# Weights in eight SP chunks cast by VectorE, add loads moved to stage 2, smaller pools: a matmul with scale and add

## The chip, the cores and the metric

The kernel runs on one core of a Trainium2 chip. Its time is device microseconds of one execution; the figures given are medians of several runs, and the profile is of one of them.

## The reference

```python
batch, m, k, n = 16, 512, 1024, 768
def reference(x, weight, scale, add_value):
    return (scale * np.matmul(x, weight) + add_value).astype(np.float32)
```

All arrays are float32, and scale is 0.1. Seen as matrices, x has 8192 rows of 1024, weight is 1024 x 768, and add_value and the output have 8192 rows of 768. So x is 33.6 MB, add_value and the output 25.2 MB each, and the weights 3.1 MB.

## The kernel before

The 8192 rows are 64 blocks of 128, handled in 32 pairs (`B = 2`). Row block b of pair i takes every 64th row, so that each of the 128 partitions reads one run of 8 KB of x for a pair, and one of 6 KB of add_value.

For each pair there are two stages. `stage1` (L102) issues the load of x on SP (L109) and that of add_value on ScalarE's queue (L111). For each of the two blocks VectorE casts x to bf16 (L119), PE transposes it in eight tiles of 128 x 128 into PSUM (L126), and ScalarE moves them to `xt`, four at a time, multiplying by scale (L132). `stage2` (L135) multiplies: for each block PE runs 8 slices of K times two parts of N (512 and 256 columns) into `mm_psum` (L143), VectorE adds `add_t` (L151), and POOL's queue stores the pair (L156).

The loop (L158) calls stage 1 of pair i and then stage 2 of pair i-2 (`DELAY`). The weights come by one transfer on POOL's queue which also casts to bf16, ahead of everything (L70); all product matmuls read this one tile.

How far one engine can run ahead of another is set by the pools: five buffers of a pair each for x, add_value and the output (`XF`, `ADD`, `OUT`), five of a block each for the bf16 x and for `xt` (`XC`, `XT`), two PSUM tiles for transposes and three for products. The order on each engine is worked out by a scheduler from the program and the pools. It puts casts and transposes ahead of the matmuls of an earlier pair, as far as buffers let it. Each engine then works strictly in that order.

Of the kernel before, what the change touches and what calls it, by code (L numbers as in the profile page):

```python
# [2 lines left out]

# [5 lines left out]


@with_exitstack
def kernel(
    ctx: ExitStack,
    tc: tile.TileContext,
    x: bass.AP,
    weight: bass.AP,
    scale: float,
    add_value: bass.AP,
    out: bass.AP,
):  # L20
# [15 lines left out]
    mm_dtype = mybir.dt.bfloat16  # L36

    B = int(os.environ.get("MB", 2))
    XF_BUFS = int(os.environ.get("XF", 5))
    XC_BUFS = int(os.environ.get("XC", 5))  # L40
    XT_BUFS = int(os.environ.get("XT", 5))
    ADD_BUFS = int(os.environ.get("ADD", 5))
    OUT_BUFS = int(os.environ.get("OUT", 5))
    TG = int(os.environ.get("TG", 4))
    SPLIT = int(os.environ.get("SPLIT", 512))
    MM_BUFS = int(os.environ.get("MMB", 3))
    DELAY = int(os.environ.get("DELAY", 2))
    XENG = os.environ.get("XENG", "sync")
    ADDENG = os.environ.get("ADDENG", "scalar")
    OUTENG = os.environ.get("OUTENG", "gpsimd")  # L50
    XCAST = int(os.environ.get("XCAST", 0))
# [10 lines left out]
    identity = const_pool.tile([P, P], mm_dtype)  # L62
    make_identity(nc, identity)

    def eng(name):
        return getattr(nc, name)

    w_view = weight.rearrange("(ko p) n -> p ko n", p=P)
    w_bf16 = const_pool.tile([P, K_SUB, N], mm_dtype)
    nc.gpsimd.dma_start(w_bf16, w_view)  # L70

    xf_pool = ctx.enter_context(tc.tile_pool(name="xf_pool", bufs=XF_BUFS))
    xc_pool = ctx.enter_context(tc.tile_pool(name="xc_pool", bufs=XC_BUFS))
    xt_pool = ctx.enter_context(tc.tile_pool(name="xt_pool", bufs=XT_BUFS))
    add_pool = ctx.enter_context(tc.tile_pool(name="add_pool", bufs=ADD_BUFS))
    out_pool = ctx.enter_context(tc.tile_pool(name="out_pool", bufs=OUT_BUFS))
    psum_t = ctx.enter_context(tc.tile_pool(name="psum_t", bufs=2, space=bass.MemoryType.PSUM))
# [18 lines left out]
    assert o <= PSUM_N  # L96

    xt_tiles = {}
    add_tiles = {}
    fscale = float(scale)  # L100

    def stage1(bi):  # L102
        b0 = bi * B
        if XCAST:
            x_all_bf16 = xf_pool.tile([P, B, K], mm_dtype, tag="x_fp32")
            nc.gpsimd.dma_start(x_all_bf16, x_v[:, b0:b0 + B, :])
        else:
            x_fp32 = xf_pool.tile([P, B, K], mybir.dt.float32, tag="x_fp32")
            eng(XENG).dma_start(x_fp32, x_v[:, b0:b0 + B, :])  # L109
        add_t = add_pool.tile([P, B, N], mybir.dt.float32, tag="add_t")  # L110
        eng(ADDENG).dma_start(add_t, add_v[:, b0:b0 + B, :])  # L111
        add_tiles[bi] = add_t

        for b in range(B):
            if XCAST:
                x_bf16 = x_all_bf16[:, b, :]
            else:
                x_bf16 = xc_pool.tile([P, K], mm_dtype, tag="x_bf16")
                nc.vector.tensor_copy(x_bf16, x_fp32[:, b, :])  # L119

            xt = xt_pool.tile([P, K_SUB, P], mm_dtype, tag="xt")
            for tg in range(T_TILES):
                tpsum = psum_t.tile([P, TG, P], mm_dtype, tag="tpsum")
                for j in range(TG):
                    kt = tg * TG + j
                    nc.tensor.transpose(  # L126
                        tpsum[:, j, :],
                        x_bf16[:, kt * P:(kt + 1) * P],
                        identity,
                    )  # L130
                dst = xt[:, tg * TG:(tg + 1) * TG, :]
                nc.scalar.mul(dst, tpsum, fscale)  # L132
            xt_tiles[(bi, b)] = xt
# [64 lines left out]
```

## Time and profile before

| | us |
|---|---|
| median of 6 runs (254.44 to 255.05) | 254.66 |
| the profiled execution | 255.05 |
| its span, first to last instruction | 253.1 |
| PE busy | 205.8 |
| VectorE busy | 106.9 |
| ScalarE busy | 71.1 |
| weights: transfer under way | 1.31 to 40.1 |

The execution's time is 1.95 us above its span. In the profile's names, PE is the matmul engine, PEld its weight loads, DVE is VectorE, ACT ScalarE, POOL GpSimd, and SP the engine that issues the loads of x; an engine's name with q is its queue. L143 is line 143 of the kernel as printed above. DMA share is the mean busy share of 16 DMA engines; it can go over 1, as packets overlap.

### The profile page before, as it was taken

The numbers are of one execution on the slowest core, as the hardware profiler recorded it, in microseconds if no ns is written. First come the engines' busy times: TensorE is split into PE (matmuls) and PEld (weight loads), VectorE is DVE, ScalarE is ACT, GpSimd is POOL, SyncE is SP. The second block draws the span as 40 slices with busy tenths as digits, with TensorE's granted clock in tenths as the row PEclk, the third lists the DMA queues.
The fourth block names the chain that finished last, engine by engine and source line by source line (L and its number), as shares of the span: only waits on it lengthen the run. The fifth ranks groups of instructions, "written<-read, shape, count | busy, mean of one in ns | idle before, by whom it ended". The sixth has DMA issues, their size and how long they took to land.

```text
span 253.1 us, 3745 instructions
## 1 busy us (share of the span) xinstructions
PE 205.8 (81%) x1506; PEld 130.7 (52%) x1536; DVE 106.9 (42%) x192; ACT 71.1 (28%) x129; POOL 18.9 (7%) x39
## 2 busy tenths in 40 slices
PE   0200006999999999999999999999999999999980
PEld 0200004666666666666666666666666666666640
DVE  0221002555555555555555555555555555433340
ACT  0400003433333333333333333333333333333000
POOL 2000000000000000000000000000000000000000
PEclk9999999999999999999999999999999999999997
DMA  7999992979999999999999999999999878863333
GB/s 258 377 378 377 370 354 82 315 238 417 372 388 420 415 417 415 416 413 419 396 403 424 413 398 414 413 388 414 418 418 412 286 246 247 246 268 124 122 130 124
DMA packets 14881, 85.70 MB, mean 339 GB/s; under 512 B 1552, under 2 KB 2576, under 8 KB 10768
## 3 DMA queue, kind: packets, MB, share of 16 engines
q1 hardware_dynamic: 4608, 33.56, 32.6%
q10 hardware_dynamic: 4608, 25.17, 27.9%
q0 software_dynamic: 5648, 26.74, 27.4%
q8 instruction: 12, 0.20, 0.3%
q14 instruction: 5, 0.04, 0.0%
HBM read 61.87 MB, written 25.17 MB: 344 GB/s over the span
## 4 chain that ended last, share of the span: by engine, by line
issue 60%; PE 17%; DMA 15%; POOL 6%; POOLq 0%; DVE 0%; DVEq 0%
DMA w_bf<-in_weight_dram 15%; PE mm_psum L143 13%; POOL out_dram L156 5%; PE tpsum L126 4%; POOLq L193 0%; DVE out_t L151 0%; POOLq L156 0%; POOL identity masks.py:197 0%; DVEq L119 0%; POOLq masks.py:199 0%; POOLq L179 0%
## 5 line engine op out<-in xcount | busy, mean ns | idle before, releaser
L143 PE MATMUL mm_psum<-w_bf,xt 128*128 128x256 bf16 (+1 forms) x994 | 181.7, 326 | 30.7 <-DMA w_bf<-in_weight_dram 29.2
L143 PEld LDWEIGHTS <-xt 128*128 128x128 bf16 x1024 | 98.0, 98 | 57.3
L132 ACT ACTIVATE xt<-tpsum 128x512 bf16<-128x512 bf16 x128 | 69.8, 594 | 154.7 <-PE tpsum L126 81.8
L151 DVE TENSOR_TENSOR out_t<-mm_psum,add_t 128x512 f32<-128x512 f32 (+1 forms) x128 | 65.4, 553 | 94.4 <-PE mm_psum L143 94.4
L126 PEld LDWEIGHTS <-x_bf 128*128 128x128 bf16 x512 | 38.1, 100 | 57.6 <-issue 44.5
L119 DVE CAST x_bf<-x_fp 128x1024 bf16<-128x1024 f32 x64 | 43.8, 689 | 45.8 <-PE tpsum L126 29.7
L126 PE MATMUL tpsum<-identity,x_bf 128*128 128x128 bf16 x512 | 46.3, 224 | 9.6 <-DVE x_bf L119 8.6
L156 POOL DMA_DIRECT2D out_dram<-out_t x32 | 17.1, 535 | 228.1 <-DVE out_t L151 228.1
L132 ACT ACT_TABLE_LOAD x1 | 1.3, 1283 | 8.4 <-DMA add_t<-in_add_value_dram 8.4
L70 POOL DMA_DIRECT2D w_bf<-in_weight_dram x1 | 1.0, 1033 | 0.4 <-issue 0.4
masks.py:199 POOL TENSOR_SCALAR_AFFINE_SELECT identity<-identity 128x128 bf16<-128x128 bf16 x1 | 0.3, 306 | 0.1
masks.py:197 POOL MEMSET identity<- 128x128 bf16 x1 | 0.2, 206 | 0.3 <-POOLq L179 0.3
L179 POOL MEMSET const-float32-0.0<- 128x1 f32 x1 | 0.1, 100 | 0.2 <-issue 0.2
L179 POOL MEMSET const-uint8-127<- 128x1 uint8 x1 | 0.1, 103 | 0.0
L179 POOL MEMSET const-bfloat16-1.0<- 128x1 bf16 x1 | 0.1, 102 | 0.0
L179 POOL MEMSET const-float32-1.0<- 128x1 f32 x1 | 0.1, 100 | 0.0
## 6 DMA issues: line engine op xcount, KB each, us to landing
x_fp<-in_x_dram SPq DMA_DIRECT2D x32, 1024.0 KB, 10.7
add_t<-in_add_value_dram ACTq DMA_DIRECT2D x32, 768.0 KB, 10.1
out_dram<-out_t POOLq DMA_DIRECT2D x32, 768.0 KB, 10.2
w_bf<-in_weight_dram POOLq DMA_DIRECT2D x1, 1536.0 KB, 38.8
```

The source lines that it names most:

```text
L70: nc.gpsimd.dma_start(w_bf16, w_view)
L119: nc.vector.tensor_copy(x_bf16, x_fp32[:, b, :])
L126: nc.tensor.transpose(tpsum[:, j, :], x_bf16[:, kt * P:(kt + 1) * P], identity,)
L132: nc.scalar.mul(dst, tpsum, fscale)
L143: nc.tensor.matmul(mm_psum[:, poffs[si]:poffs[si] + nlen], xt[:, kt, :], w_bf16[:, kt, n0:n0 + nlen], start=(kt == 0), stop=(kt == K_SUB - 1),
L151: nc.vector.tensor_add(out_t[:, b, n0:n0 + nlen], mm_psum[:, poffs[si]:poffs[si] + nlen], add_t[:, b, n0:n0 + nlen],)
L156: eng(OUTENG).dma_start(out_v[:, bi * B:(bi + 1) * B, :], out_t)
L179: nc = _bacc.Bacc("TRN2", target_bir_lowering=False, num_devices=1)
```

## The change

- Weights: the one casting transfer on POOL's queue is gone. There are eight chunks of 128 x 768 in float32, each with tiles of its own (`wf`, `wb`), loaded on SP (L89) and cast to bf16 by VectorE (L111). Chunk 0 is issued behind x of pair 0, chunks 1 to 7 behind x of pair 1.
- add_value: its load is no longer part of stage 1. `load_add` comes ahead of stage 2 of the same pair; the first three go on SP, the others on ScalarE's queue (L148).
- Pools: x from 5 to 3 buffers, bf16 x from 5 to 3, `xt` from 5 to 4, add_value from 5 to 3, output from 5 to 4.
- `DELAY` is 1 where it was 2.
- Stores of the last six pairs go on SP where the others go on POOL's queue (L211).
- Switches that are read from the environment are added; with their defaults they change nothing else.

```diff
-    XF_BUFS = int(os.environ.get("XF", 5))
-    XC_BUFS = int(os.environ.get("XC", 5))
-    XT_BUFS = int(os.environ.get("XT", 5))
-    ADD_BUFS = int(os.environ.get("ADD", 5))
-    OUT_BUFS = int(os.environ.get("OUT", 5))
...
-    DELAY = int(os.environ.get("DELAY", 2))
...
+    XF_BUFS = _env("XF", 3)
+    XT_BUFS = _env("XT", 4)
+    ADD_BUFS = _env("ADD", 3)
+    OUT_BUFS = _env("OUT", 4)
...
+    DELAY = _env("DELAY", 1)
...
-    w_bf16 = const_pool.tile([P, K_SUB, N], mm_dtype)
-    nc.gpsimd.dma_start(w_bf16, w_view)
...
+        for kt in range(K_SUB):
+            wf = const_pool.tile([P, N], fp32, tag=f"wf{kt}")
+            wb = const_pool.tile([P, N], mm_dtype, tag=f"wb{kt}")
...
+        def load_weight_chunk(kt):
+            nc.sync.dma_start(w_fp32[kt], w_view[:, kt, :])
...
+                nc.vector.tensor_copy(w_bf16[kt], w_fp32[kt])
...
-    xc_pool = ctx.enter_context(tc.tile_pool(name="xc_pool", bufs=XC_BUFS))
+    xc_pool = ctx.enter_context(tc.tile_pool(name="xc_pool", bufs=_env("XC", 3)))
...
+    def load_add(bi):
+        add_t = add_pool.tile([P, B, N], fp32, tag="add_t")
+        e = nc.sync if bi < ADD_BUFS else eng(ADDENG)
+        e.dma_start(add_t, add_v[:, bi * B:(bi + 1) * B, :])
+        add_tiles[bi] = add_t
...
-        add_t = add_pool.tile([P, B, N], mybir.dt.float32, tag="add_t")
-        eng(ADDENG).dma_start(add_t, add_v[:, b0:b0 + B, :])
-        add_tiles[bi] = add_t
...
-                        w_bf16[:, kt, n0:n0 + nlen],
+                        w_bf16[kt][:, n0:n0 + nlen],
...
+        if bi >= N_BATCH - _env("OLAST", 6):
+            oe = os.environ.get("OLASTENG", "sync")
+        eng(oe).dma_start(out_v[:, bi * B:(bi + 1) * B, :], out_t)
...
     for bi in range(N_BATCH + DELAY):
         if bi < N_BATCH:
             stage1(bi)
+            if WINTER and wk < K_SUB:
+                load_weight_chunk(wk)
+                cast_weight_chunk(wk)
+                wk += 1
         if bi >= DELAY:
-            stage2(bi - DELAY)
+            if WINTER and bi == DELAY:
+                while wk < K_SUB:
+                    load_weight_chunk(wk)
+                    cast_weight_chunk(wk)
+                    wk += 1
+            load_add(bi - DELAY)
```

On SP at the start of the program, five loads of x stood one after the other before, as many as there are buffers (`x_fp_86` is pair 0, `x_fp_120` pair 1, and so on):

```order
L109 DMA x_fp_86<-in_x_dram 128x2048
L109 DMA x_fp_120<-in_x_dram 128x2048
L109 DMA x_fp_154<-in_x_dram 128x2048
L109 DMA x_fp_228<-in_x_dram 128x2048
L109 DMA x_fp_302<-in_x_dram 128x2048
```

Now the weight chunks and three loads of add_value stand among them (`x_fp_100` is pair 0, `x_fp_134` pair 1, `x_fp_222` pair 2):

```order
L154 DMA x_fp_100<-in_x_dram 128x2048
L89 DMA wf<-in_weight_dram 128x768
L154 DMA x_fp_134<-in_x_dram 128x2048
L89 DMA wf<-in_weight_dram 128x768 x7
L148 DMA add_t<-in_add_value_dram 128x1536
L154 DMA x_fp_222<-in_x_dram 128x2048
L148 DMA add_t<-in_add_value_dram 128x1536
L154 DMA x_fp_296<-in_x_dram 128x2048
```

What moved: the third load of x stands behind all the weights and the first load of add_value, which were on other queues.

On PE at the second slice of K of the very first block, the matmul before read the one weight tile (`w_bf16_63`), as did the one ahead of it:

```order
L126 MATMUL tpsum_114<-identity_58,x_bf16_105 128x128
L143 LDWEIGHTS xt_92
L143 MATMUL mm_psum_189<-w_bf16_63,xt_92 128x256
L143 LDWEIGHTS xt_92
L143 MATMUL mm_psum_189<-w_bf16_63,xt_92 128x512
```

Now it reads a chunk of its own (`wb_64` is chunk 0, `wb_66` chunk 1):

```order
L170 MATMUL tpsum_126<-identity_58,x_bf16_117 128x128
L194 LDWEIGHTS xt_104
L194 MATMUL mm_psum_183<-wb_64,xt_104 128x256
L194 LDWEIGHTS xt_104
L194 MATMUL mm_psum_183<-wb_66,xt_104 128x512
```

The place in the row is the same; what the matmul needs is now one cast of VectorE, where it was the whole transfer.

On VectorE in the long stage, the cast of the first block of pair 14 (`x_fp32_1042`) stood ahead of the adds of pair 9 (`out_t_854`):

```order
L119 CAST x_bf16_987<-x_fp32_968 128x1024
L119 CAST x_bf16_1046<-x_fp32_1042 128x1024
L151 TENSOR_TENSOR out_t_854<-mm_psum_855,add_t_674 128x512
L151 TENSOR_TENSOR out_t_854<-mm_psum_855,add_t_674 128x256
L151 TENSOR_TENSOR out_t_854<-mm_psum_874,add_t_674 128x512
```

Now it is the cast of the first block of pair 8 (`x_fp32_666`) that stands ahead of the adds of pair 5 (`out_t_552`):

```order
L159 CAST x_bf16_609<-x_fp32_592 128x1024
L159 CAST x_bf16_668<-x_fp32_666 128x1024
L202 TENSOR_TENSOR out_t_552<-mm_psum_553,add_t_550 128x512
L202 TENSOR_TENSOR out_t_552<-mm_psum_553,add_t_550 128x256
L202 TENSOR_TENSOR out_t_552<-mm_psum_572,add_t_550 128x512
```

The row is of the same kind; the casts now lead the adds by three pairs where they led by five.

## Rows read from the trace of the kernel before

**Rows 1.** The page: its span, PE's busy time, and PE in 40 slices
```profile
span 253.1 us, 3745 instructions
...
PE 205.8 (81%) x1506; PEld 130.7 (52%) x1536; DVE 106.9 (42%) x192; ACT 71.1 (28%) x129; POOL 18.9 (7%) x39
...
PE   0200006999999999999999999999999999999980
```

**Rows 2.** The chain of waits: start us, us, what
```profile
1.31 38.80 DMA w_bf<-in_weight_dram
40.14 0.59 PE mm_psum L143
40.73 0.43 PE tpsum L126 x4
...
50.36 0.45 PE tpsum L126 x8
...
141.17 0.53 POOL out_dram L156
...
147.56 0.53 POOL out_dram L156
...
237.02 0.53 POOL out_dram L156
...
242.23 0.53 POOL out_dram L156
```

**Rows 3.** Waits: who for whom, us in total, times, longest
```profile
PE mm_psum L143 <- DMA w_bf<-in_weight_dram: 29.2, 1, 29.2
```

**Rows 4.** Windows: stretch, its us, busy by engine, clock, DMA share, GB/s
```profile
0.00:4.00 4.00, 0.00 (x0) 0.00 (x0) 0.00 (x0) 0.00 (x0) 1.75 (x7) 1.00 0.55 164
4.00:6.00 2.00, 0.00 (x0) 0.00 (x0) 0.00 (x0) 0.00 (x0) 0.00 (x0) 1.00 1.02 424
10.00:40.00 30.00, 0.58 (x4) 0.42 (x4) 2.59 (x4) 1.40 (x3) 0.00 (x0) 1.00 1.03 363
32.00:36.00 4.00, 0.00 (x0) 0.00 (x0) 0.00 (x0) 0.00 (x0) 0.00 (x0) 1.00 1.04 342
56.00:66.00 10.00, 9.90 (x78) 6.31 (x79) 5.66 (x10) 3.26 (x6) 1.07 (x2) 1.00 1.02 421
80.00:200.00 120.00, 118.96 (x889) 75.54 (x904) 63.14 (x114) 41.06 (x76) 10.15 (x19) 1.00 1.01 408
```

**Rows 5.** Waits of SP's queue: us in total, times, longest
```profile
SPq L109 <- DVE x_bf L119: 154.3, 26, 19.2
```

**Rows 6.** Timeline of the start: start us, us, engine, line, operation, idle before
```profile
7.88 1.29 DVE L119 CAST x_bf<-x_fp 128x1024 bf16<-128x1024 f32 x2 [7.88 <-DMA x_fp<-in_x_dram]
```

**Rows 7.** The page: DMA queues q1 (x), q10 (add_value), and the casts of x
```profile
q1 hardware_dynamic: 4608, 33.56, 32.6%
q10 hardware_dynamic: 4608, 25.17, 27.9%
...
L119 DVE CAST x_bf<-x_fp 128x1024 bf16<-128x1024 f32 x64 | 43.8, 689 | 45.8 <-PE tpsum L126 29.7
```

**Rows 8.** Timeline of the last 8 us
```profile
246.10 1.02 DVE L151 TENSOR_TENSOR out_t<-mm_psum,add_t 128x512 f32<-128x512 f32 x2 [1.58 <-PE mm_psum L143]
247.42 0.53 POOL L156 DMA_DIRECT2D out_dram<-out_t  x1 [4.67 <-DVE out_t L151]
```

**Rows 9.** DMA queues in 248 to 252 us: packets, MB, share
```profile
q0 software_dynamic: 144, 0.79, 48.2%
```

**Rows 10.** DMA issues in 80 to 120 us: KB each, median us to landing
```profile
x_fp<-in_x_dram SPq DMA_DIRECT2D x6, 1024.0 KB, 10.1
add_t<-in_add_value_dram ACTq DMA_DIRECT2D x6, 768.0 KB, 9.6
```

**Rows 11.** DMA issues in 0 to 10 us
```profile
x_fp<-in_x_dram SPq DMA_DIRECT2D x5, 1024.0 KB, 17.1
```

**Rows 12.** DMA packets in 10 to 40 us
```profile
DMA packets 2374, 10.88 MB, mean 363 GB/s; under 512 B 192, under 2 KB 1106, under 8 KB 1553
```

More of the change, by code (lines that the diff above doesn't have):

```diff
@@ L50 @@
     OUTENG = os.environ.get("OUTENG", "gpsimd")
-    XCAST = int(os.environ.get("XCAST", 0))
+    TCEV = os.environ.get("TCEV", "scalar")
+    WCAST = os.environ.get("WCAST", "vector")
+    WSCALE = _env("WSCALE", 0)
+    WCHUNK = _env("WCHUNK", 1)
     assert M_TILES % B == 0
@@ L60 @@
     const_pool = ctx.enter_context(tc.tile_pool(name="const", bufs=1))
-    identity = const_pool.tile([P, P], mm_dtype)
+    XBF = _env("XBF", 1)
+    identity = const_pool.tile([P, P], mm_dtype if XBF else fp32)
     make_identity(nc, identity)
@@ L66, in eng, with load_weight_chunk, cast_weight_chunk @@
         return getattr(nc, name)
+    fscale = float(scale)
     w_view = weight.rearrange("(ko p) n -> p ko n", p=P)
-    w_bf16 = const_pool.tile([P, K_SUB, N], mm_dtype)
-    nc.gpsimd.dma_start(w_bf16, w_view)
+    w_bf16 = []
+    w_fp32 = []
+    if WCHUNK:
+        for kt in range(K_SUB):
+            wf = const_pool.tile([P, N], fp32, tag=f"wf{kt}")
+            wb = const_pool.tile([P, N], mm_dtype, tag=f"wb{kt}")
+            w_fp32.append(wf)
+            w_bf16.append(wb)
+        def load_weight_chunk(kt):
+            nc.sync.dma_start(w_fp32[kt], w_view[:, kt, :])
+    else:
+        wf = const_pool.tile([P, K_SUB, N], fp32, tag="wf")
+        wb = const_pool.tile([P, K_SUB, N], mm_dtype, tag="wb")
+        for kt in range(K_SUB):
+            w_fp32.append(wf[:, kt, :])
+            w_bf16.append(wb[:, kt, :])
+        nc.sync.dma_start(wf, w_view)
+        def load_weight_chunk(kt):
+            pass
+    def cast_weight_chunk(kt):
+        if WCAST == "scalar":
+            nc.scalar.mul(w_bf16[kt], w_fp32[kt], fscale if WSCALE else 1.0)
+        elif WCAST == "gpsimd":
+            nc.gpsimd.tensor_copy(w_bf16[kt], w_fp32[kt])
+        else:
+            if WSCALE:
+                nc.vector.tensor_single_scalar(
+                    w_bf16[kt], w_fp32[kt], fscale, op=mybir.AluOpType.mult)
+            else:
+                nc.vector.tensor_copy(w_bf16[kt], w_fp32[kt])
     xf_pool = ctx.enter_context(tc.tile_pool(name="xf_pool", bufs=XF_BUFS))
-    xc_pool = ctx.enter_context(tc.tile_pool(name="xc_pool", bufs=XC_BUFS))
+    xc_pool = ctx.enter_context(tc.tile_pool(name="xc_pool", bufs=_env("XC", 3)))
     xt_pool = ctx.enter_context(tc.tile_pool(name="xt_pool", bufs=XT_BUFS))
@@ L76 @@
     out_pool = ctx.enter_context(tc.tile_pool(name="out_pool", bufs=OUT_BUFS))
-    psum_t = ctx.enter_context(tc.tile_pool(name="psum_t", bufs=2, space=bass.MemoryType.PSUM))
+    psum_t = ctx.enter_context(tc.tile_pool(name="psum_t", bufs=T_BUFS, space=bass.MemoryType.PSUM))
     psum_mm = ctx.enter_context(tc.tile_pool(name="psum_mm", bufs=MM_BUFS, space=bass.MemoryType.PSUM))
@@ L81 @@
     T_TILES = K_SUB // TG
+    SPLIT = 512
     splits = []
@@ L99 @@
     add_tiles = {}
-    fscale = float(scale)
+    evict_mul = 1.0 if WSCALE else fscale
+    def load_add(bi):
[3 more added lines that the diff above has]
+        add_tiles[bi] = add_t
     def stage1(bi):
         b0 = bi * B
[L104 to L109, printed above, removed]
-        add_t = add_pool.tile([P, B, N], mybir.dt.float32, tag="add_t")
-        eng(ADDENG).dma_start(add_t, add_v[:, b0:b0 + B, :])
-        add_tiles[bi] = add_t
+        x_fp32 = xf_pool.tile([P, B, K], fp32, tag="x_fp32")
+        eng(XENG).dma_start(x_fp32, x_v[:, b0:b0 + B, :])
         for b in range(B):
-            if XCAST:
-                x_bf16 = x_all_bf16[:, b, :]
-            else:
+            if XBF:
                 x_bf16 = xc_pool.tile([P, K], mm_dtype, tag="x_bf16")
                 nc.vector.tensor_copy(x_bf16, x_fp32[:, b, :])
+                t_in = x_bf16
+                t_dt = mm_dtype
+            else:
+                t_in = x_fp32[:, b, :]
+                t_dt = fp32
             xt = xt_pool.tile([P, K_SUB, P], mm_dtype, tag="xt")
             for tg in range(T_TILES):
-                tpsum = psum_t.tile([P, TG, P], mm_dtype, tag="tpsum")
+                tpsum = psum_t.tile([P, TG, P], t_dt, tag="tpsum")
                 for j in range(TG):
@@ L131, in stage1 @@
                 dst = xt[:, tg * TG:(tg + 1) * TG, :]
-                nc.scalar.mul(dst, tpsum, fscale)
+                if TCEV == "scalar":
+                    nc.scalar.mul(dst, tpsum, evict_mul)
+                else:
+                    if evict_mul == 1.0:
+                        eng(TCEV).tensor_copy(dst, tpsum)
+                    else:
+                        eng(TCEV).tensor_single_scalar(
+                            dst, tpsum, evict_mul, op=mybir.AluOpType.mult)
             xt_tiles[(bi, b)] = xt
@@ L136, in stage2 @@
         add_t = add_tiles.pop(bi)
-        out_t = out_pool.tile([P, B, N], mybir.dt.float32, tag="out_t")
+        out_t = out_pool.tile([P, B, N], fp32, tag="out_t")
         for b in range(B):
             xt = xt_tiles.pop((bi, b))
-            mm_psum = psum_mm.tile([P, PSUM_N], mybir.dt.float32, tag="mm_psum")
+            mm_psum = psum_mm.tile([P, PSUM_N], fp32, tag="mm_psum")
             for kt in range(K_SUB):
@@ L155, in stage2 @@
                 )
-        eng(OUTENG).dma_start(out_v[:, bi * B:(bi + 1) * B, :], out_t)
+        oengs = OUTENG.split(",")
+        oe = oengs[bi % len(oengs)]
+        if bi >= N_BATCH - _env("OLAST", 6):
+            oe = os.environ.get("OLASTENG", "sync")
+        eng(oe).dma_start(out_v[:, bi * B:(bi + 1) * B, :], out_t)
+    WINTER = _env("WINTER", 1)
+    if not WINTER:
+        for kt in range(K_SUB):
+            load_weight_chunk(kt)
+        for kt in range(K_SUB):
+            cast_weight_chunk(kt)
+    GRP = _env("GRP", 1)
+    wk = 0
+    done2 = 0
     for bi in range(N_BATCH + DELAY):
```

18 lines of the change are left out of this document (13 added, 5 removed).

## The prediction

> **What bounds the kernel now.** I read the page first: the span is 253.1 us and PE is busy 205.8 of it [rows 1]. Its forty slices are nearly empty up to the seventh and full from there to the end, so there are two stages: a start of 40 us without product matmuls, and a long stage in which PE is the bound. The chain of waits names the start: one transfer, the weights, from 1.31 us for 38.80 us, and then the first product matmul at 40.14 [rows 2]. The table of waits says the same: PE waited 29.2 us for w_bf, once [rows 3]. In the long stage the stores start every 6.39 us (141.17, 147.56), one pair of row blocks each. The last pairs have no transposes and come 5.20 us apart (237.02, 242.23) [rows 2].
>
> The second thing to see is how near DMA is to being a bound. A pair moves 1.049 MB of x, 0.786 MB of add_value and 0.786 MB of output: 2.62 MB in 6.39 us, 410 GB/s. The windows show 408 GB/s over 80 to 200 us at a DMA share of 1.01, and 421 GB/s over 56 to 66 us, when it was catching up [rows 4]. SP nevertheless waited 154.3 us for VectorE to free x buffers [rows 5], so DMA kept up and PE set the pace, with a margin of some 3% (421 against 410).
>
> **The start.** Before, the weights shared the engines with ten prefetched loads. Now everything early goes through SP in one line: x of pair 0, weight chunk 0, x of pair 1, chunks 1 to 7, and only then add_value. What counts is when PE stops waiting. The order shows its product matmuls with the first chunk, transposes, and then a matmul on the second chunk (wb_66). On VectorE the cast of that chunk stands behind the two casts of x of pair 1.
> - Bytes up to x of pair 1: 1.049 + 0.393 + 1.049 = 2.49 MB; chunk 1 makes it 2.88 MB. In 0 to 4 us the trace moved 0.66 MB, and then 424 GB/s [rows 4], a line that begins at 2.45 us. With half a microsecond for completion (an estimate: the first cast starts at 7.88 [rows 6], when 2.2 MB have moved, and its load, its equal beside it and the weights' share are about 2.0), x of pair 1 lands at 8.8 us and chunk 1 at 9.8.
> - Casts of x take 689 ns each [rows 7]: 8.8 + 1.4 = 10.2 us. A chunk has three quarters of the elements, 0.52 us: PE goes on at 10.7 us. At 375 GB/s it would be 12.0.
> - From there PE's work is that of before from 40.14 us, less four transposes and two matmuls already done (0.43 + 0.43 + 0.21 = 1.07 us at the early rate [rows 2]). The shift is 40.14 - 10.7 + 1.07 = 30.5 us.
> - Later chunks come every 0.93 us and are each cast in 0.52. PE needs them more slowly, since it starts at the low rate: four transposes take 0.43 us at 40.73 us and eight take 0.45 at 50.36 [rows 2], that is 107 and 56 ns for 128 columns, the 1.2 and the 2.4 GHz level, after 29 us of idle (the clock column reads 1.00 for this stretch all the same). The order has three tiles under way by then, so the seven casts hide behind PE. That warm-up was paid before as well and cancels.
>
> PE alone would give a span of 253.1 - 30.5 = 222.6 us.
>
> **The new wait.** Before, DMA had until 40 us to fill five x and five add buffers. Now PE starts when next to nothing is prefetched, with three of each. On VectorE, which works in order, the cast of x five pairs ahead stood before the adds of a pair; now it is the cast three pairs ahead. Queued behind a late x are thus the adds, behind these the PSUM buffers, and PE waits for those. I follow pair 8. On the schedule of PE alone the last adds end at 247.1 - 30.5 = 216.6 us (before: 246.10 + 1.02 [rows 8]); pair 31 starts 5.2 + 1.0 us earlier, at 210.4, and pair 6 starts 25 x 6.39 us before that, at 50.65. The adds of pair 5 must free PSUM for the second tile of pair 6, which starts 3.8 us in (1.2 of transposes and 2.6 of product). With 1.0 us of adds and 0.7 of cast before, x of pair 8 must be there at 52.7. By then DMA has to have moved the weights (3.15 MB), x of nine pairs (9.44), about 7.5 add loads (5.90, since they are issued two pairs ahead) and 4.8 stores (3.77): 22.3 MB.
> - At 421 GB/s from 2.95 us: 55.8 us, a stall of 3.1. Each pair then takes 6.22 us on DMA, under 6.39, so it does not grow.
> - At 410: 57.2 us, 4.5 us late, and it stays so.
> - At 400: 5.9 us late, and growing by 0.16 us a pair over the 23 pairs left that need x, some 10 us.
> - If only the loads then due (adds of 0 to 5, stores of 0 to 3, 20.4 MB) went ahead: 51.4 us, no stall.
>
> I take 4 us, between the first two, as 408 and 421 are both read from full queues [rows 4]; the ends are 0 and 10.
>
> **Smaller terms.** A weight chunk has rows of 3 KB; x has 8 KB and add_value 6 KB. 4608 packets of x took 32.6% and 4608 of add_value 27.9% [rows 7]; a straight line through these gives 20.9% for 3 KB, 239 GB/s, and the 3.15 MB of weights would take 13.2 us in place of 7.5. So 0 to +5.7 us, on the stall only. But the last store, with 6 KB rows and alone, moved 0.79 MB in 48.2% of 4 us [rows 9], 409 GB/s, as fast as the mix, so row size is nearer to nothing: +1.
>
> The two loops that got shorter cost nothing by themselves. An add load is issued behind two evictions of its batch, some 1.5 us into pair i, for the adds of pair i+2 at 2 x 6.39 + 3.8: 15 us, against 9.6 to landing [rows 10]. An x load is issued when the second cast of pair i+3 ends, at about i's start + 8.1, and its successor is cast first at + 20.9: 12.8 us against 10.1 [rows 10], and 6.7 more before PE feels it. Stores have four periods. Without that cover each microsecond over it would be lost per pair.
>
> The last six stores move from POOL to SP, where all x loads are done. The tail before is 247.42 to 253.1 us [rows 8]; I leave it, at 0, give or take 0.5.
>
> **Sum.** 222.6 + 4 + 1 = 227.6 us span. The profiled execution took 255.05 us, 1.95 over its span, and the median is 0.39 below it: 227.6 + 1.95 - 0.39 = 229.2. I say 229.
>
> **The rivals.**
> *PE alone.* DMA catches up within the start, because VectorE's slack and the idle PSUM take the stall up. For it: 424 GB/s at 4 to 6 us and 421 later [rows 4]. 222.6 + 1.56 = 224.2, or 222.5 if PE's clock rises earlier through the short bursts from 6 us on.
> *DMA becomes the bound throughout.* Three buffers can't ride over dips, and DMA gives 400 GB/s on average: 222.6 + 10 + 1 + 1.56 = 235; with PE dropping to its low clock once in such a gap, 2.5 us more. For it: the share was already 1.01. Against: 408 was what PE asked for, with SP waiting for buffers.
> *The start is not freed.* If the first loads land as late as before, 17.1 us after issue [rows 11], though fewer are in line, chunk 1's cast ends at 19.8 us: 9.1 us later, 233.3, and the DMA stall hides in it.
> *Slower than before.* One mechanism: DMA runs as slowly as in the first stage, and PE starves. The last x load is due for pair 29, by when 22.3 + 23 x 2.62 = 82.5 MB have to have moved. At the 363 GB/s of 10 to 40 us [rows 4] they take 227.3 us, pair 29 starts at 2.95 + 227.3 - 2.05 = 228.2, and from there it is 19.0 us to the last add, 6.0 to the end of the span and 1.56 to the median: 254.8, so 363 is the point from which it decides. At the 342 GB/s of 32 to 36 us [rows 4] it would be 268.7. Against it: in that stretch 1106 of 2374 packets were under 2 KB [rows 12], from the weights' casting load, which the change takes out.
> The Trainium skill ("DMA: Bandwidth & Descriptors", Specifications) gives about 358 GB/s of HBM bandwidth for each core, below what this kernel asks; by that rule the time would be some 258 us. The trace disagrees: 408 GB/s over 120 us on a core that runs alone. The same page's fabric ceiling of 435 GB/s stands only just over the 421, which agrees with the thin margin.
>
> **How the numbers follow.** Forecast (a stall of 2 to 8 us in all, 226 to 232.5): 0.55. PE alone (222.5 to 226): 0.18. DMA throughout (232.5 to 238): 0.17. Start not freed: 0.05. Slower: 0.05. The range reaches down through the second case and up through most of the third and the fourth: 222.5 to 237. About 0.2% is what can be told from no change here; nothing but the last case ends near or above 254.66, and I leave 0.01 for a tie: faster 0.94, same 0.01, slower 0.05.
>
> **What would show it.** PE continuous from 10 to 12 us; a product-matmul wait on VectorE's weight casts, none on DMA; DMA near 420 GB/s from 4 us to the last x load; VectorE's casts waiting for x loads, a few us in all and mostly before 70 us; then a period of 6.39 us between stores. Wrong it would be if PE paused beyond 70 us at every pair (DMA throughout), if the first product matmuls came after 18 us, or if casts never waited for x.

## The result, and the profile after

The changed kernel takes 226.21 us (median of 8 runs, 225.69 to 227.56). Over all the sessions the kernel before took 254.85 us. The ratio is 0.8877, 95% interval [0.886, 0.8894]: 28.6 us less. The profiled execution took 226.9 us, 1.9 over its span.

The page of the kernel after, its span, PE's busy time, and PE and DMA's rate in 40 slices (of 5.6 us):

```profile
span 225.0 us, 3765 instructions
...
PE 204.7 (91%) x1507; PEld 130.2 (58%) x1536; DVE 108.2 (48%) x200; ACT 71.1 (32%) x129; POOL 15.5 (7%) x32
...
PE   0599887699999999999999999999999999999990
...
GB/s 242 420 409 425 414 428 424 425 422 392 395 424 425 425 422 425 424 425 422 426 424 427 427 418 430 423 422 425 427 410 421 425 415 420 390 299 280 143 140 140
```

Against [rows 1] the empty slices have shrunk to one. A dip has appeared in the fifth to eighth slice (22 to 45 us): 8, 8, 7, 6 tenths. PE's work itself is as before (204.7 against 205.8 us).

The start, from the timeline (start us, us, engine, line, operation, idle before and its releaser):

```profile
5.46 1.29 DVE L159 CAST x_bf<-x_fp 128x1024 bf16<-128x1024 f32 x2 [5.46 <-DMA x_fp<-in_x_dram]
...
8.91 1.29 DVE L159 CAST x_bf<-x_fp 128x1024 bf16<-128x1024 f32 x2 [1.69 <-DMA x_fp<-in_x_dram]
...
10.73 0.59 PE L194 MATMUL mm_psum<-wb,xt 128*128 128x512 bf16 x1 [1.57 <-DVE wb L111]
```

The first cast comes at 5.46 us where it came at 7.88 [rows 6]. PE takes up the second chunk at 10.73 us; before, the product matmuls began at 40.14 [rows 2]. The 29.2 us of [rows 3] have become 1.57.

The dip, from the same view, VectorE and PE at 31 to 55 us:

```profile
31.00 2.11 PE L194 MATMUL mm_psum<-wb,xt 128*128 128x256 bf16 x11
...
34.45 1.29 DVE L159 CAST x_bf<-x_fp 128x1024 bf16<-128x1024 f32 x2 [2.89 <-DMA x_fp<-in_x_dram]
...
35.20 0.62 PE L170 MATMUL tpsum<-identity,x_bf 128*128 128x128 bf16 x8 [2.09 <-DVE x_bf L159]
...
40.58 1.29 DVE L159 CAST x_bf<-x_fp 128x1024 bf16<-128x1024 f32 x2 [3.27 <-DMA x_fp<-in_x_dram]
...
41.34 0.62 PE L170 MATMUL tpsum<-identity,x_bf 128*128 128x128 bf16 x8 [2.03 <-DVE x_bf L159]
...
51.75 0.69 DVE L159 CAST x_bf<-x_fp 128x1024 bf16<-128x1024 f32 x1 [3.46 <-DMA x_fp<-in_x_dram]
52.36 1.01 DVE L202 TENSOR_TENSOR out_t<-mm_psum,add_t 128x512 f32<-128x512 f32 x2
...
54.49 0.87 PE L170 MATMUL tpsum<-identity,x_bf 128*128 128x128 bf16 x8 [0.21 <-ACT xt L177]
```

Two blocks are cast for a pair, so counting casts from the start gives the pairs: 34.45 is pair 4, 40.58 pair 5, 51.75 pair 7. PE ran out of work at 33.1 us and waited 2.09 us for the transposes of pair 4, and 2.03 for those of pair 5. At pair 7 the adds stand behind the late cast, as the prediction had it for pair 8, but of that PE feels 0.21 us.

Windows of the same stretch (stretch, its us, busy PE, PEld, DVE, ACT, POOL with counts, clock, DMA share, GB/s), and the long stage:

```profile
20.00:24.00 4.00, 3.67 (x28) 2.35 (x27) 4.00 (x9) 0.45 (x1) 1.01 (x1) 1.00 1.03 424
24.00:28.00 4.00, 3.70 (x28) 2.46 (x29) 1.58 (x3) 1.72 (x4) 0.53 (x1) 1.00 1.01 415
28.00:32.00 4.00, 3.95 (x36) 2.72 (x36) 2.04 (x4) 2.17 (x4) 0.14 (x1) 1.00 1.01 426
32.00:36.00 4.00, 1.91 (x18) 1.14 (x17) 1.29 (x2) 0.30 (x1) 0.39 (x1) 1.00 1.01 426
36.00:40.00 4.00, 3.30 (x26) 2.00 (x24) 1.02 (x2) 1.87 (x4) 0.00 (x0) 1.00 1.01 425
40.00:50.00 10.00, 8.42 (x69) 5.61 (x72) 4.45 (x8) 3.26 (x6) 0.53 (x1) 1.00 1.01 422
50.00:60.00 10.00, 9.64 (x69) 6.01 (x68) 6.91 (x13) 3.26 (x6) 1.56 (x2) 1.00 1.00 392
...
80.00:200.00 120.00, 118.91 (x887) 75.49 (x904) 62.82 (x116) 41.26 (x76) 9.06 (x17) 1.00 1.01 419
```

From 20 to 60 us PE is busy 34.59 of 40 us. The long stage leaves it idle for 1% (118.91 of 120), so the stall of this execution is 5.41 - 0.36 = 5.05 us (it differs from one execution to another, see e7). All through it DMA moves 415 to 426 GB/s, but for the last window, with its share at 1.0: it gives what it can. From 60 us on nothing is lost; the chain of waits (start us, us, what) shows the period of 6.39 us again:

```profile
14.82 19.54 DMA x_fp<-in_x_dram
...
61.04 0.45 PE tpsum L170 x8
...
67.43 0.45 PE tpsum L170 x8
```

The first line is the load of x for pair 4: 19.54 us from issue to landing, where the prediction counted with 10.1 [rows 10].

At the end, from the timeline, the last adds end at 219.64 + 1.02 = 220.66 us and the span at 225.0, so the tail is 4.3 us; before it was 6.0 (247.12 to 253.1, [rows 1, 8]):

```profile
219.64 1.02 DVE L202 TENSOR_TENSOR out_t<-mm_psum,add_t 128x512 f32<-128x512 f32 x2 [1.58 <-PE mm_psum L194]
```

### The profile page after: what moved, and what is told of

Its sections match the earlier page's. It is cut to its first block, busy times and chain, and to the rows that moved or that the text cites. A ratio compares the mean times of both kernels' runs of the same rounds, so it can differ in the third digit from the quotient of the medians.

```text
span 225.0 us, 3765 instructions
## 1 busy us (share of the span) xinstructions
PE 204.7 (91%) x1507; PEld 130.2 (58%) x1536; DVE 108.2 (48%) x200; ACT 71.1 (32%) x129; POOL 15.5 (7%) x32
## 4 chain that ended last, share of the span: by engine, by line
PE 72%; DMA 22%; DVE 1%; issue 1%; ACT 1%; DVEq 0%; ACTq 0%; SPq 0%
PE mm_psum L194 59%; DMA x_fp<-in_x_dram 18%; PE tpsum L170 13%; DMA wf<-in_weight_dram 4%; DVE out_t L202 1%; ACT xt L177 1%; DVE x_bf L159 1%; ACTq L148 0%; DVEq L272 0%; DVEq L159 0%; ACTq L177 0%; SPq L154 0%
## 5 line engine op out<-in xcount | busy, mean ns | idle before, releaser
L194 PE MATMUL mm_psum<-wb,xt 128*128 128x256 bf16 (+1 forms) x995 | 180.7, 326 | 2.9 <-DVE wb L111 1.6
L202 DVE TENSOR_TENSOR out_t<-mm_psum,add_t 128x512 f32<-128x512 f32 (+1 forms) x128 | 64.4, 551 | 44.5 <-PE mm_psum L194 43.5
L159 DVE CAST x_bf<-x_fp 128x1024 bf16<-128x1024 f32 x64 | 43.4, 688 | 65.6 <-DMA x_fp<-in_x_dram 61.5
L170 PE MATMUL tpsum<-identity,x_bf 128*128 128x128 bf16 x512 | 46.0, 223 | 11.9 <-DVE x_bf L159 10.3
L170 PEld LDWEIGHTS <-x_bf 128*128 128x128 bf16 x512 | 37.6, 100 | 31.8 <-issue 16.0
L211 POOL DMA_DIRECT2D out_dram<-out_t x26 | 14.8, 570 | 168.2 <-DVE out_t L202 168.2
L111 DVE CAST wb<-wf 128x768 bf16<-128x768 f32 x8 | 4.5, 558 | 2.3 <-DMA wf<-in_weight_dram 2.3
## 6 DMA issues: line engine op xcount, KB each, us to landing
out_dram<-out_t POOLq DMA_DIRECT2D x26, 768.0 KB, 13.9
add_t<-in_add_value_dram SPq DMA_DIRECT2D x3, 768.0 KB, 11.1
```

Source lines behind the costliest of these rows:

```text
L111: nc.vector.tensor_copy(w_bf16[kt], w_fp32[kt])
L170: nc.tensor.transpose(tpsum[:, j, :], t_in[:, kt * P:(kt + 1) * P], identity,)
L194: nc.tensor.matmul(mm_psum[:, poffs[si]:poffs[si] + nlen], xt[:, kt, :], w_bf16[kt][:, n0:n0 + nlen], start=(kt == 0), stop=(kt == K_SUB - 1),
L202: nc.vector.tensor_add(out_t[:, b, n0:n0 + nlen], mm_psum[:, poffs[si]:poffs[si] + nlen], add_t[:, b, n0:n0 + nlen],)
L211: eng(oe).dma_start(out_v[:, bi * B:(bi + 1) * B, :], out_t)
```

## The experiments

Twelve kernels ran; each is the changed kernel with one edit, but for e9, which is the kernel before with one edit, and e10 to e12, which build on e8. Times are medians, ratios are to the kernel before on the same chip. "Last adds" is when the last adds end in the profile, "tail" what follows to the end of the span.

| run | edit | us | ratio, 95% | last adds | tail |
|---|---|---|---|---|---|
| after | | 226.21 | 0.8877 [0.886, 0.8894] | 220.66 | 4.3 |
| e1 | last stores on POOL | 227.44 | 0.8918 [0.8892, 0.8944] | 219.43 | 6.0 |
| e2 | one add load | 223.47 | 0.877 [0.8746, 0.8793] | 216.58 | 4.6 |
| e3 | add loads in stage 1 | 229.57 | 0.9005 [0.8975, 0.9036] | 222.66 | 4.3 |
| e4 | weights in one casting load | 242.91 | 0.9531 [0.9508, 0.9554] | 235.28 | 4.7 |
| e5 | five buffers everywhere | 230.36 | 0.9068 [0.904, 0.9096] | 223.61 | 4.3 |
| e6 | two buffers of bf16 x | 225.77 | 0.8874 [0.8816, 0.8932] | 220.10 | 4.3 |
| e7 | PE warmed first | 228.89 | 0.9006 [0.8958, 0.9053] | 222.74 | 4.3 |
| e8 | stores held, six ahead | 223.02 | 0.8777 [0.8757, 0.8797] | 217.27 | 4.3 |
| e9 | before, weights in chunks | 236.82 | 0.9291 [0.924, 0.9342] | 227.94 | 6.0 |
| e10 | e8, last store split | 222.36 | 0.8717 [0.8702, 0.8731] | 216.68 | 3.3 |
| e11 | e8, five ahead | 222.32 | 0.8716 [0.8703, 0.8729] | 216.55 | 4.4 |
| e12 | e10 and e11 | 221.51 | 0.8705 [0.8684, 0.8727] | 216.32 | 3.4 |

### Is the dip want of bytes? (e2, e8, e11)

e2 loads add_value for pair 0 alone and uses it for all:

```diff
-        add_t = add_pool.tile([P, B, N], fp32, tag="add_t")
+        if bi > 0:
+            add_tiles[bi] = add_tiles["one"]
+            return
+        add_t = const_pool.tile([P, B, N], fp32, tag="add_one")
+        add_tiles["one"] = add_t
```

> Only pair 0's add_value is loaded, and added to every pair (24.4 MB of loads are left out), all else as in the changed kernel. Theory: the 5 us that PE loses between 23 and 60 us are DMA's bytes; without the add loads they vanish, VectorE's casts hardly wait for x beyond the first pairs, and the time is 221 (range 220.3 to 222). Rival: three x buffers and the shorter lead make the loss through the latency of a load and not through bytes; then most of it stays and the time is 225 to 226.

It took 223.47 us, 2.5 above what was expected. The mechanism did as expected, the size did not. The table of waits (who for whom, us in total, times, longest), two rows of e2 and then the same two of after:

```profile
DVE x_bf L163 <- DMA x_fp<-in_x_dram: 8.9, 3, 5.7
PE tpsum L174 <- DVE x_bf L163: 6.5, 1, 6.5
...
DVE x_bf L159 <- DMA x_fp<-in_x_dram: 61.5, 24, 5.5
PE tpsum L170 <- DVE x_bf L159: 10.3, 3, 6.2
```

Of the 8.9 us 5.7 are the first load, and PE waits for a cast only once, at the first one. The last adds end at 216.58 us; the prediction's schedule of PE alone had 216.6. So the dip is DMA's. (e2 also takes the add loads off ScalarE's queue; e8 leaves them there.) The expected time was too low, since PE's own schedule leaves nothing earlier to be had: the other runs without the dip end there too (e11, 216.55).

e8 keeps all bytes but moves some of them back. A store waits until x six pairs further on has been cast; eight output buffers make room. A small operation of POOL makes the link, adding zero times an element of that x to one column of the output:

```diff
+                if b == 0 and bi - HOLD in held:
+                    out_h = held.pop(bi - HOLD)
+                    z = z_pool.tile([P, 1], fp32, tag="z")
+                    nc.gpsimd.tensor_single_scalar(
+                        z, x_bf16[:, 0:1], 0.0, op=mybir.AluOpType.mult)
+                    nc.gpsimd.tensor_add(out_h[:, 0, 0:1], out_h[:, 0, 0:1], z)
+                    nc.gpsimd.dma_start(out_v[:, (bi - HOLD) * B:(bi - HOLD + 1) * B, :], out_h)
...
-        eng(oe).dma_start(out_v[:, bi * B:(bi + 1) * B, :], out_t)
+        if bi + HOLD < N_BATCH:
+            held[bi] = out_t
+        else:
+            eng(oe).dma_start(out_v[:, bi * B:(bi + 1) * B, :], out_t)
```

> The changed kernel with each store held back by two pairs: a small operation on POOL, which reads the bf16 x of the pair six ahead and adds 0 times it to one column of the output tile, stands ahead of the store; eight output buffers. Theory: 1.57 MB of stores less are moved by the time x of a pair is due, 3.7 us at 424 GB/s, and the DMA has the time for them at the end, when the x loads are done; the stall nearly vanishes and the time is 223 to 224.5. Rival (held stores come in the way of loads later on, or the last ones lengthen the tail): 226 or more.

Measured: 223.02 us, and PE's waits for casts of x are down to the first one (6.3 us). e11 sets `HOLD` to 5 where e8 has 6:

> Stores held back by one pair instead of two. Theory: 0.79 MB less is moved by the time x of pairs 4 and 5 is due, 1.9 us of the 4 us that PE waited for it, and the time is 224 to 225, between 226.2 and 223.0. Rival (it is the presence of a store beside the x loads that matters, not the bytes): either 226 or 223.

It took 222.32, faster than either expectation. e12, below, has the same hold. Windows of e12 over two stretches that lost much in after:

```profile
32.00:36.00 4.00, 4.00 (x37) 2.72 (x36) 2.62 (x6) 2.14 (x5) 0.00 (x0) 1.00 1.01 420
...
40.00:50.00 10.00, 9.80 (x71) 6.18 (x70) 3.98 (x8) 2.31 (x5) 2.54 (x6) 1.00 1.01 419
```

and the casts of pairs 4 and 5 in its timeline:

```profile
31.96 1.28 DVE L163 CAST x_bf<-x_fp 128x1024 bf16<-128x1024 f32 x2
...
35.56 1.28 DVE L163 CAST x_bf<-x_fp 128x1024 bf16<-128x1024 f32 x2
```

The casts come 2.5 and 5.0 us earlier than in after, at the same rate of DMA. The loads were not issued earlier (14.9 and 22.9 us, in after 14.8 and 22.4); they took 15.7 and 12.1 us to land where they took 19.5 and 18.1. In after 1.26 MB of stores had moved when x of pair 4 landed at 34.4 us, and 2.05 MB when x of pair 5 did at 40.5, 3.0 and 4.9 us at 420 GB/s; in e12 the first store is issued at 37.5 us. So a `HOLD` of 5 puts every store of this stretch behind x, not one of 0.79 MB as the theory of e11 had it, and a `HOLD` of 6 brought no more.

### Is it the lead of the casts? (e6, e5)

e6 has two buffers of bf16 x where after has three, so that a cast leads by less and fewer adds stand behind it.

```diff
-    xc_pool = ctx.enter_context(tc.tile_pool(name="xc_pool", bufs=_env("XC", 3)))
+    xc_pool = ctx.enter_context(tc.tile_pool(name="xc_pool", bufs=_env("XC", 2)))
```

> The changed kernel with two buffers of bf16 x where it has three: the cast of x stands two pairs ahead of the adds. Theory: one x load fewer is due at the same moment, 1.05 MB or 2.5 us, so most of the stall is gone and the time is 223.5 to 225. Rival (the shorter lead exposes each load's latency, or the extra wait of the casts for the transposes): 226.5 or more.

The theory fell: 225.77 us, no difference that can be told from after. VectorE's own waits for x sank from 61.5 to 23.1 us, but those of PE for VectorE's casts were 10.3 in 3, to the tenth those of after. Not the adds behind the cast but the cast itself was what PE waited for.

e5 goes the other way, with five buffers of everything:

```diff
-    XF_BUFS = _env("XF", 3)
-    XT_BUFS = _env("XT", 4)
-    ADD_BUFS = _env("ADD", 3)
-    OUT_BUFS = _env("OUT", 4)
+    XF_BUFS = _env("XF", 5)
+    XT_BUFS = _env("XT", 5)
+    ADD_BUFS = _env("ADD", 5)
+    OUT_BUFS = _env("OUT", 5)
```

(and five of bf16 x; the first three add loads stay on SP).

> The changed kernel with the pools of before: five buffers for x, bf16 x, xt, add_value and output. Theory (DMA's bytes due before PE may go on): on VectorE the cast of x then stands four pairs ahead of the adds where it stood three, and the add loads run three pairs ahead where it was two; 1.05 + 0.79 MB more are due at the same moment, 4.3 us at 424 GB/s, so the time rises to 229 to 231. Rival (deeper buffers cover more latency): 224 to 226.2. It also tells what the smaller pools are worth in the change.

230.36 us, as expected, and here the prediction's chain can be seen but for one link. The timeline of e5:

```profile
50.66 1.30 DVE L159 CAST x_bf<-x_fp 128x1024 bf16<-128x1024 f32 x2 [3.93 <-DMA x_fp<-in_x_dram]
51.87 1.02 DVE L202 TENSOR_TENSOR out_t<-mm_psum,add_t 128x512 f32<-128x512 f32 x2
52.92 0.34 ACTq L148 DMA_DIRECT2D add_t<-in_add_value_dram  x1
...
53.30 1.08 ACT L177 ACTIVATE xt<-tpsum 128x512 bf16<-128x512 bf16 x2 [6.88 <-DVE out_t L202]
53.95 0.58 PE L170 MATMUL tpsum<-identity,x_bf 128*128 128x128 bf16 x4 [4.71 <-ACT xt L177]
```

A late cast, then the adds queued behind it. These free the add buffer for which ScalarE's add load has been waiting, and with that load ScalarE's evictions; PE waits 4.71 us for them. The adds did not reach PE through PSUM, as the prediction said, but through ScalarE, whose queue holds the add loads. The windows of e5 show a second cost:

```profile
50.00:52.00 2.00, 0.00 (x0) 0.00 (x0) 1.34 (x3) 0.00 (x0) 0.00 (x0) 1.00 1.03 432
...
54.00:56.00 2.00, 2.00 (x9) 1.09 (x9) 0.59 (x1) 0.98 (x2) 0.00 (x0) 0.50 1.03 431
```

After that wait PE works at a granted clock of 0.50, the 1.2 GHz level, and does 9 matmuls in 2 us.

### What freed the start? (e4, e9, e3, e7)

e4 brings the weights in one casting load on POOL's queue, as before the change, and keeps the rest of the change:

```diff
+        w_all = const_pool.tile([P, K_SUB, N], mm_dtype, tag="w_all")
+        nc.gpsimd.dma_start(w_all, w_view)
+        w_bf16 = [w_all[:, kt, :] for kt in range(K_SUB)]
...
-            nc.sync.dma_start(w_fp32[kt], w_view[:, kt, :])
```

> The weights come again by one casting transfer on POOL's queue; the add loads' place, pools, DELAY and last stores stay as changed. Theory (the small packets of the casting transfer take their turns among the others', 65 rounds of them per DMA engine, whatever the number of loads ahead): the first product matmul at 27 to 33 us, no stall for x after it, and 240 to 246 us. Rival (it was the ten prefetched loads that held the weights back, not the transfer itself): first product matmul before 20 us and 228 to 233 us.

242.91 us. The chain of e4, its first pieces:

```profile
1.30 27.70 DMA w_all<-in_weight_dram
29.05 0.59 PE mm_psum L196
```

and its window from 4 to 26 us, while that transfer was under way:

```profile
4.00:26.00 22.00, 1.62 (x12) 1.30 (x13) 2.59 (x4) 1.68 (x3) 0.00 (x0) 1.00 1.06 353
```

The first product matmul starts 18.3 us later than PE's second chunk in after, and DMA moves 353 GB/s at a share of 1.06. Over the same stretch of after it is 415. The low rate of [rows 4] goes with the casting load. The transfer took 27.7 us where it took 38.8 in before [rows 2], so the loads beside it count as well, other than the theory had it. As PE starts late, x is never short in e4, and 3.3 of the 18.3 us come back: its span is 240.0 us.

e9 is the kernel before with the weights alone in chunks, issued on SP behind x of pairs 0 and 1:

```diff
-    w_bf16 = const_pool.tile([P, K_SUB, N], mm_dtype)
-    nc.gpsimd.dma_start(w_bf16, w_view)
+    def weight_chunk(kt):
+        nc.sync.dma_start(w_fp32[kt], w_view[:, kt, :])
+        nc.vector.tensor_copy(w_bf16[kt], w_fp32[kt])
...
+            for kt in {0: [0], 1: range(1, K_SUB)}.get(bi, []):
+                weight_chunk(kt)
```

> The kernel before with the weights alone changed: eight chunks on SP, chunk 0 behind x of pair 0 and the others behind x of pair 1, cast by VectorE; five buffers everywhere, add loads in stage 1, DELAY 2 and stores on POOL's queue as before. Theory: five add loads and the deep pools move more bytes ahead of those that are due; PE starts its steady work at 16 to 19 us, the last adds end at 224 to 227, the tail is 6 us, and the time 231 to 236. Rival (the weights' way is the whole gain, and the rest of the change costs or does nothing): 225 to 228.5.

236.82 us, a little over the theory's range, so chunks alone are not the change. Its timeline:

```profile
18.03 0.58 PE L151 MATMUL mm_psum<-wb,xt 128*128 128x512 bf16 x1 [6.02 <-DVE wb L78]
...
22.32 3.78 PE L151 MATMUL mm_psum<-wb,xt 128*128 128x512 bf16 x13 [2.00 <-DVE wb L78]
```

PE gets its second chunk at 18.03 us and is held up once more until 22.32, while loads of add_value share DMA: four of them stand first on ScalarE's queue, and the first piece of the chain of e9 is one of them, from 0.74 us. The 28.1 us between the spans of before and after can now be parted. The last adds come 19.2 us earlier in e9 than in before (227.94 against 247.12), and 7.3 us earlier again in after (220.66): add loads out of the start, less prefetch and `DELAY`, taken together. The other 1.65 is the tail.

e3 undoes one of these alone and issues the add loads in stage 1, on ScalarE's queue:

```diff
-        e = nc.sync if bi < ADD_BUFS else eng(ADDENG)
+        e = eng(ADDENG)
...
         eng(XENG).dma_start(x_fp32, x_v[:, b0:b0 + B, :])
+        load_add(bi)
...
-            load_add(bi - DELAY)
```

> The add loads go back into stage 1 on ScalarE's queue; chunks, pools and DELAY stay as changed. Three add loads then run beside x and chunk 0 from the first microsecond. Theory (bytes due by pair 8 set PE's pace, and they are the same): PE's steady work begins 3 to 5 us later, at 14 to 16 us, but the stall shrinks by about as much, and the time is 226 to 228. Rival (the start of PE sets the time, the stall is added to it): 229.5 to 231.

229.57 us: the theory, 226 to 228, fell. The timeline of e3:

```profile
16.59 0.58 PE L195 MATMUL mm_psum<-wb,xt 128*128 128x512 bf16 x1 [4.35 <-DVE wb L111]
```

PE took up the second chunk at 16.59 us, 5.9 later, yet the last adds came only 2.0 later. They end at 222.66, which is 216.6 + 5.9 + 0.2: PE's own schedule, moved by the later start, and little of the dip is left (from 20 to 60 us PE is busy 39.6 of 40 us, in after 34.6). So the late start and the dip do not add up; the time goes by whichever of PE's schedule and DMA's is later.

e7 lets PE do 44 transposes of the identity before its first work, to have it at its high clock by then:

```diff
+    for r in range(11):
+        tpsum = psum_t.tile([P, TG, P], mm_dtype, tag="tpsum")
+        for j in range(TG):
+            nc.tensor.transpose(tpsum[:, j, :], identity, identity)
```

> The changed kernel with 44 transposes of the identity ahead of everything on PE, between 1.4 and 6 us where it is idle; nobody reads their results. Theory: PE's low clock at the start is hidden behind DMA (its last adds would come up to 2.5 us earlier by themselves, but x isn't there), so the time stays within 0.7 us of 226.2. Rival (PE's work from 10.7 us on sets the time): 224 to 225.

Both expectations fell: 228.89 us. Windows of e7, and two lines of its timeline:

```profile
8.00:9.00 1.00, 0.60 (x6) 0.32 (x5) 0.00 (x1) 1.00 (x3) 0.00 (x0) 1.00 0.94 381
...
11.00:12.00 1.00, 1.00 (x10) 0.93 (x9) 1.00 (x2) 0.36 (x1) 0.00 (x0) 0.50 1.02 399
...
38.00:40.00 2.00, 2.00 (x14) 1.37 (x12) 0.43 (x2) 0.88 (x2) 0.53 (x1) 0.50 1.03 431
...
36.14 0.69 DVE L159 CAST x_bf<-x_fp 128x1024 bf16<-128x1024 f32 x1 [4.70 <-DMA x_fp<-in_x_dram]
36.89 0.62 PE L170 MATMUL tpsum<-identity,x_bf 128*128 128x128 bf16 x8 [3.77 <-DVE x_bf L159]
```

PE was at its high rate by 7.6 us (four transposes in 0.38 us in the timeline), ended at 8.6, waited 1.99 us for the second chunk, and went on at 0.50. So e7 does not show what a fast PE from 10.7 us on would be worth. The wait for pair 4 is one of 3.77 us, and the clock falls to 0.50 behind it too.

Why x of pair 4 came later than in after can be read beside e1 (below), whose program is that of after but for the last six stores. Two lines of the timeline of e1, then one of after:

```profile
22.68 1.01 POOL L211 DMA_DIRECT2D out_dram<-out_t  x1 [21.37 <-DVE out_t L202]
32.64 1.28 DVE L159 CAST x_bf<-x_fp 128x1024 bf16<-128x1024 f32 x2
...
21.52 1.01 POOL L211 DMA_DIRECT2D out_dram<-out_t  x1 [20.21 <-DVE out_t L202]
```

| | e1 | after | e7 |
|---|---|---|---|
| x of pair 4 issued, us | 14.8 | 14.8 | 14.9 |
| first store issued, us | 22.7 | 21.5 | 20.7 |
| x of pair 4, issue to landing, us | 17.2 | 19.5 | 21.1 |
| stores, and add loads on ScalarE's queue, moved by that landing, MB | 1.05 | 2.05 | 2.6 |
| PE idle from 20 to 60 us | 2.7 | 5.4 | 4.4, and at 0.50 for a part |
| last adds end, us | 219.43 | 220.66 | 222.74 |

The sooner PE delivers its first products, the sooner stores and new add loads share DMA with the x that PE will wait for, and the later that x lands. PE in e1 worked longer at the low rate at the start, and ended earlier. These are single profiles; e8 and e11, which take the stores out of the stretch, fit them, with 15.2 and 15.7 us for the same load. So the dip of after, too, is that of one execution.

### The tail (e1, e10, e12)

e1 puts the last six stores on POOL's queue again:

```diff
-        if bi >= N_BATCH - _env("OLAST", 6):
+        if bi >= N_BATCH - _env("OLAST", 0):
```

> The changed kernel with the last six stores on POOL's queue again. Theory: the tail from the last add to the end of the span, 6.0 us before and 4.3 us after, is the store's queue; it goes back to about 6.0 and the time to 227.9 (+1.7). Rival: the tail got shorter because DMA is emptier at the end in the changed kernel; then the tail stays at 4.3 and the time at 226.2.

The timeline of e1 at its end (its span is 225.4 us):

```profile
218.41 1.02 DVE L202 TENSOR_TENSOR out_t<-mm_psum,add_t 128x512 f32<-128x512 f32 x2 [1.58 <-PE mm_psum L194]
```

The tail is 5.97 us, that of before, and 1.63 more than in after. The last adds came 1.2 us earlier in this profile, as its dip was smaller (see e7). The time, 227.44 us, lies 1.2 higher, but the two intervals overlap. That the last store on SP ends sooner is shown by the profiles; what it is worth in the median is 1 to 1.6 us by these runs and not known better.

e10 is e8 with the store of the last pair split, one for each block:

```diff
+            for b in range(B):
+                eng(oe).dma_start(out_v[:, bi * B + b, :], out_t[:, b, :])
```

> The kernel with stores held back by two pairs, with the last pair stored one block at a time. Theory: the last store is half as long and the first half of the pair leaves 2.6 us earlier, so the tail shrinks by 0.39 MB at 424 GB/s, 0.9 us, and the time is 222 to 222.4 where it was 223.0. Rival (the tail is fixed cost of a store's completion): 223.

222.36 us against 223.02, with the tail at 3.3 us. (The last adds, too, come 0.6 us earlier in this profile than in that of e8, which the split does not explain.) e12 puts the split and the shorter hold of e11 together:

> The run that held each store for one pair (last adds ending at 216.55 us, tail 4.35) and the one that stored the last pair as two blocks (tail 3.3) put together. Theory: the two gains are independent, since one is the start's DMA and the other the end's: last adds at 216.6, tail 3.3, span 219.9, and with the 1.4 to 2.4 us that lay above the spans of those two, 221.3 to 222.3; I take 221.6. Rival: what lies above the span absorbs the tail's gain, as it did by half when the stores were held for two pairs: no less than 222.3, as the one pair's hold alone.

221.51 us, ratio 0.8705 [0.8684, 0.8727]; its span is 219.7. That is the lowest time of all, 4.7 us under the changed kernel. Against e10 and e11 it isn't told apart by the intervals, but its last adds (216.32) and its tail (3.4) are where the two gains together put them.

## Why the prediction was right, and where it was not

The time is 226.21 us where 229 was forecast. It lies 0.2 us inside the lower edge of the likeliest case (a stall of 2 to 8 us, 226 to 232.5), and the mechanism, PE waiting in its early pairs for bytes that DMA has not moved yet, is that case's. By the steps:

- **The start.** x of pair 1 was forecast to land at 8.8 us and is cast at 8.91; PE was to go on at 10.7 and did at 10.73. The later casts hide behind PE as forecast. The schedule of PE alone, last adds at 216.6, was then met by the runs in which DMA no longer held PE up: 216.58 (e2) and 216.55 (e11). Some of this is pieces that cancel: in both PE went on at 11.0, the clock rose earlier than in before (below), and some 0.6 us were lost between 20 and 28 us.
- **The new wait, its size.** 4 us were taken, and 1 for the short rows. Measured: 5.05 us of PE's idle time in after, with the last adds 4.1 us behind the 216.6 of PE alone, and 2.7 and 2.8 us in e1, with the same start. With the hold of e11 the last adds come at 216.55. The two terms together are of the right size; in part that is luck, as they were counted for a pair at which PE was not stopped. Apart, the rows of the weights cost less than 1: in after the chunks are cast 0.98 us apart, where the prediction counted 0.93, which is 0.4 us over eight.
- **The new wait, its place.** This step failed. The prediction followed pair 8 through adds and PSUM and let x be due at 52.7 us. PE was stopped at 33.1 us, at the transposes of pair 4, then at those of pair 5. PE's transposes of pair 4 came due at 33.1, its cast some 0.75 earlier (34.45 to 35.20), at 32.4; x landed at 34.4, 2 us late, the 2.09 of the row. DMA had moved 13.4 MB by then: 11.3 on SP's queue, of which five loads of x, the weights and three add loads, which end with x of pair 4, are 10.75, and 1.3 of stores and 0.8 of add loads on ScalarE's queue. Counted in the prediction's way, at 421 GB/s from 2.95 us, the 10.75 MB alone would have landed at 28.5 us, in time, and with the two stores and two add loads issued by 26 us wholly ahead of them, 13.9 MB, at 36.0, 3.6 us late. The balance had to be made for every pair, not for one in the middle, and the share that stores and add loads take decides it.
- **The way to PE.** The adds behind a late cast do reach PE (4.71 us in e5, 1.33 in e1, 0.21 in after), but through the add load on ScalarE's queue, not through PSUM.
- **The clock at the start.** It was taken to cancel. Four transposes take 0.63 us at the low rate and 0.39 at the high one; in before they go on at 0.63 from 40.5 to 45.2 us, in after from 11.1 to 13.5. So PE worked low for 5.1 us then and for 2.8 now, half of the difference, 1.15 us of work, ahead. No run shows that this was gained; a PE that is ahead waits the longer for x. In e1, e5, e8 and e10 to e12 the four transposes at 13.7 to 14.0 us still took 0.63, so the moment varies from run to run, and of e1 and after, e1 has its last adds earlier.
- **The tail.** Taken at 0, give or take 0.5; it gave 1.65. This was the term that was most mis-sized against its own bounds. What a store on another queue costs at the end had no row in before, and I bounded it too narrowly.
- **The sum.** 216.6 + 5.05 - 1.15 = 220.5 for the last adds, 220.66 measured; and 4.34 of tail gives the span of 225.0. Against the forecast the last adds are 0.9 us earlier, the tail is 1.65 shorter, and the median lies 1.2 us above the profile's span where 1.56 were taken: together the 3 us between 229.2 and 226.2.
- **The rivals.** DMA was no bound throughout: the period is 6.39 us from 61 us on. DMA moved 419 GB/s over 80 to 200 us, so the 408 of [rows 4], which the forecast took for the rate of full queues, was what PE asked for. PE alone did not come in after, but the runs without the dip (e2, e8, e11) took 222.3 to 223.5, about where that rival put the time. The mechanism of the slower rival did not come: the low rate of DMA returned only with the casting load of e4 (353). The Trainium skill ("DMA: Bandwidth & Descriptors", Specifications) gives some 358 GB/s for a core, half of what the two cores of a memory stack share; as a limit for this one core the trace disagrees, with 419 here and 424 at 80 to 180 us in e11. Its fabric ceiling of 435 agrees: the highest of the 40 slices is 430.
- **What was to show it** did: PE on from 10.7 us, its only product wait on VectorE's cast of a chunk (1.57 us), the pauses over before 70 us, then the period of 6.39.

What stays open: why the clock rose at 13.5 us in some runs (after, e2) and later in others; how far the order of e1, after and e7, one profile each, would hold over many; and how the 7.3 us between e9 and after part between the pools, `DELAY` and the order of the add loads; e3 alone undoes 2.0 of them.

## What to carry to other kernels

When a start is freed, count the bytes due and the bytes possible for each of the first tiles, at the rate that the profile shows with full queues; where DMA has only some per cent to spare, what matters is which bytes go first, and a store that can wait should. A stall in the start and a later start do not add: the time goes by the later of the two schedules (e3). Work that only makes PE ready sooner can even lose while data is late, where its stores and next loads then go ahead of that data (e1, after and e7 suggest it; e8 and e11 show the gain of holding stores). At the end, look at how long the last store takes from the last add on, by queue and by size.

## What the runs showed of the hardware

- A casting load of the weights lowers what all DMA moves: 353 GB/s at a share of 1.06 while it ran (e4), against 415 in the same stretch, 4 to 26 us, without it (after).
- TensorE's granted clock fell to 0.50, the 1.2 GHz level, when PE went on after idle time of 4.71 us (e5), 3.77 us and 1.99 us (e7, the last one at 8.6 us). After the two waits of about 2 us in after, at 33 and 39 us, it stayed at 1.00.
- The tail from the last adds to the end of the span was 6.0 us with the last store of 0.79 MB on POOL's queue, 4.3 to 4.7 with it on SP's, and 3.3 to 3.4 with its second half alone left to store.
- In the long stage loads of x took a median of 15.1 us from issue to landing in after, 10.1 before [rows 10], with DMA moving 419 and 408 GB/s over 80 to 200 us. In the start the load of x for pair 4 took 19.5 us with 2.05 MB of stores and add loads moved beside it on other queues, and 15.7 us without stores (e11).
